# A fifth place for raw weights, paid for with the memory of the first norm's two vectors

## The chip, the cores and the metric

The kernel runs on one core of a Trainium2 chip. The metric is the device time of one execution in microseconds (us), as the median over runs. The engines are named as in the profile: PE is TensorE (PEld its weight loads), DVE VectorE, ACT ScalarE, POOL GpSimd, SP SyncE, which here does little but issue transfers. `L302` is line 302 of the kernel before.

## The reference

One decoder layer on 512 tokens of width 1024 in float32, cut to what matters:

```python
f = swiglu(rms_norm(h, ffn1_norm_pre), gate1, up1, down1)      # 1024 -> 2816 -> 1024
h = h + 0.5 * rms_norm(f, ffn1_norm_post)
u = rms_norm(h, mix_norm_pre)
q, k, v, xr, yr, gl = split(u @ w_in)                          # 12 heads of 128; LRU width 1024
attn = dilated_window_attention(q, k, v)                       # 3 groups of 4 heads, mixed by log-sum-exp
rec = rg_lru(causal_conv4(xr)) * gelu(yr)                      # two gates, 4 blocks of 256x256
merged = sigmoid(gl_0) * (attn @ w_attn_branch) + sigmoid(gl_1) * (rec @ w_rec_branch)
h = h + rms_norm(merged @ w_out, mix_norm_post)
f = swiglu(rms_norm(h, ffn2_norm_pre), gate2, up2, down2)
h = h + 0.5 * rms_norm(f, ffn2_norm_post)
```

## The kernel before

**Products.** A float32 product is made of three matmuls on operands that are split into a high and a low part: high times high, high times low, low times high (`mm3`, L314 to L317). The large products use a seven-product form in the manner of Strassen: sums of weight quarters and of activation quarters are multiplied in products p1 to p7. `seventh` (L709 to L717) issues such products with 128x256 matmuls L715, L716, L717; the feed-forward's down projection issues them with 128x512 matmuls L966, L967, L968 in `down7`, called S matmuls below.

**Weights.** All weights come as raw float32 tiles of 128x1024 from one stream `in_w`. `raw_of` (L234) takes a place with the tag `raw`, of which there are four, and SP issues the transfer (L242). A raw tile is split by `split`: ScalarE copies out the high part (L302), VectorE subtracts it to get the low part (L303). For the seven-product form `w_forms` (L671) and `w_forms_within` (L691) make sums first: L678, L679, L680 and L683 on VectorE, some of them in place in the raw tile; `d_forms` (L893) does the same for the down projection, L909 to L923. A raw place is free again when its last split has been done.

**Feed-forward.** The 22 blocks of the hidden width are computed in order, the first ones (six in the first feed-forward, three in the second) in the standard form (`std_out`, L853, which in the first feed-forward scales by the norm's vector `r1` on the way out), the others in the seven-product form. For the down projection they are cut into five parts of four, four, four, four and six blocks. The first four, a0 to a3, use the seven-product form; the last is multiplied in the ordinary way. The down projection of each of a0 to a3 goes in four steps i0 to i3, interleaved with the gate and up products of the next blocks (`prod`, L866). A step i computes the products `SEVEN_STEPS[i]`: p1 and p7; p4 and p6; p5; p2 and p3. `down7` (L957) collects each in one of three `aux` banks of PSUM, ScalarE first puts the chain sum into the bank (`seed`, L955) where one exists, and evacuates it (L971) into `facc` or into `ea`, a tile `[128, 4, 2, 512]` with the tag `e` of the pool `act1`, which `seed` allocates (L951). `copy` (L729) evacuates the gate and up products.

**Mixer.** Each of four head indices has three heads (one of each dilation). Their scores use an exchange by matmul (L1314), transposes (L1340, L1358, L1363) and softmax operations on VectorE and ScalarE (L1343, L1349, L1352), interleaved with the next products (operands `rb`). In the recurrence the convolution is L1466 and L1469, the gate's two products are L315 and L316 on `rec`, and the gating is L1541 to L1543.

**Order.** A framework schedules the program at build: it fixes one order for each engine from the program's order, priorities and the number of places of each tag. `tc.high_priority(offset=AHEAD)` (100) pulls raw transfers, sums and splits ahead, `EVAC` (200) evacuations. So a place more for a tag changes the built order of engines, not only the waits in it. At run time each engine keeps its order and waits on semaphores.

**First norm.** `acc` (sum of squares) and `r1` (the reciprocal root) are two tiles `[128, 512]` of a pool of their own, `npool`. The first weight block (k = 0) of the start lands in the left part of `first_t`, whose right part `sm` holds small vectors; the blocks k = 1 to 7 land in the halves of four raw places, in which the left half of the first stays empty (`fetch_start`, L277).

Of the kernel before, what the change touches and what calls it, by code (L numbers as in the profile page):

```python
# [10 lines left out]
F32 = mybir.dt.float32  # L11
# [5 lines left out]
P = 128  # L17
T = 512
# [11 lines left out]
EPS = 1e-6  # L30
HB = 256
RAW_W = 1024
NEG = -1.0e30

FIRST_ON = {1: 5, 2: 5}
# [67 lines left out]
def stream_plan():  # L103

    plan = []

    def down(n, a, half):
        for kk in range(part_blocks(a)):
            plan.append((("down", n, a, half, kk), 1024))

    def ffn(n):
        for ev in ffn_order(n):
            if ev[0] == "std":
                plan.append((("gate", n, ev[1]), 1024))
                plan.append((("up", n, ev[1]), 1024))
            elif ev[0] == "prep":
                plan.append((("gu", n, ev[1]), 2048))
            elif ev[0] == "prepd":
                for q in SEVEN_RAW[ev[2]]:
                    plan.append((("dq", n, ev[1], q), 1024))  # L120
        for half in range(2):
            down(n, len(FF_PARTS) - 1, half)

    def qk(h):
        for g in range(NG):
            plan.append((("pair", g * 4 + h, 12 + g * 4 + h), 2048))

    ffn(1)
    del plan[:4]
    for k in range(KC):  # L130
        plan.insert(k, (("start", k), 512))
    for k in range(4):
        plan.append((("v", 0, k), 1024))
    for q in ("g0", "g1", "u0", "u1"):
        plan.append((("vq", q), 2048))
    for h in range(NH):
        qk(h)
    for c in range(0, KC, 2):
        plan.append((("pair", 52 + c, 53 + c), 2048))
    for m in range(0, KC, 2):  # L140
        plan.append((("attn", m), 1024))
    for what, h in LRU_ORDER:
        if what == "gates":
            plan.append((("lru", h), 1024))
        elif (what, h) in PAIRED:
            plan.append((pair_key(what, h), 2048))
        else:
            for c in GATE1[h] if what == "gate1" else (2 * h, 2 * h + 1):
                plan.append((("in", COLUMN[what] + c), 1024))
    for m in range(KC):  # L150
        plan.append((("rec", m), 1024))
    for half in range(2):
        for kk in range(4):
            plan.append((("out", half, kk), 1024))
    ffn(2)

    return [(key + (i,), RAW_W) if width > RAW_W else (key, width)
            for key, width in plan for i in (("lo", "hi") if width > RAW_W else ("",))]


def stream_groups():

    groups, cur, w = [], [], 0
    for key, width in stream_plan():
        if w + width > RAW_W or (cur and cur[0][0][0] == "start"):
            groups.append(cur)
# [12 lines left out]
SMALL_W = _o  # L179
# [4 lines left out]
def hybrid_layer(ctx: ExitStack, tc: tile.TileContext, xT: bass.AP, xN: bass.AP, wst: bass.AP,  # L184
# [4 lines left out]
    cpool = ctx.enter_context(tc.tile_pool(name="cpool", bufs=1))  # L189
    bpool = ctx.enter_context(tc.tile_pool(name="bpool", bufs=6))  # L190
    wpool = ctx.enter_context(tc.tile_pool(name="wpool", bufs=4))
    tpool = ctx.enter_context(tc.tile_pool(name="tpool", bufs=4))
    npool = ctx.enter_context(tc.tile_pool(name="npool", bufs=1))
    psum = ctx.enter_context(tc.tile_pool(name="psum", bufs=1, space=bass.MemoryType.PSUM))
    dpool = ctx.enter_context(tc.tile_pool(name="dpool", bufs=1, space=bass.MemoryType.DRAM))

    first_t = cpool.tile([P, 512 + SMALL_W], F32, name="first")
    sm = first_t[:, 512:]
    cst = cpool.tile([P, CONST_W], F32, name="cst")
    ones = cpool.tile([P, P], F32, name="ones")  # L200
    eps = cpool.tile([P, 1], F32, name="eps")
# [6 lines left out]
    def hm(m, sl=slice(0, T)):  # L208

        return hs["t"][m // 4][:, m % 4, sl]  # L210
# [23 lines left out]
    def raw_of(key, dst=None):  # L234

        g, i = state["g"], state["i"]
        grp = groups[g]
        if i == 0:
            w = grp[-1][1] + grp[-1][2]
            raw = dst if dst is not None else wpool.tile([P, RAW_W], F32, name="raw", tag="raw", bufs=4)  # L240
            src = bass.AP(tensor=wst.tensor, offset=wst.offset + state["off"], ap=[[w, P], [1, w]])
            nc.sync.dma_start(raw[:, :w], src)  # L242
            state["raw"] = raw
            state["off"] += w * P
        k, o, w = grp[i]
        assert k == key, (k, key)
        src = state["raw"][:, o:o + w]
        if i + 1 == len(grp):
            state["g"], state["i"] = g + 1, 0
        else:  # L250
            state["i"] = i + 1
        return src

    def raw_two(key, dst=None):

        return [raw_of(key + (n,), None if dst is None else dst[:, i * RAW_W:(i + 1) * RAW_W])
                for i, n in enumerate(("lo", "hi"))]

    def fetch(key, slot=None, ahead=0):

        with tc.high_priority(offset=ahead if slot else state["ahead"]):
            src = raw_of(key)
            w = src.shape[-1]
            t = slot() if slot else w8() if w > 512 else w4()
            split(t[:, 0, :w], t[:, 1, :w], src)
            return t[:, 0, :w], t[:, 1, :w]

    def w8():
        return wpool.tile([P, 2, 1024], F32R, name="w8", tag="w8", bufs=4)
# [6 lines left out]

    def fetch_start():  # L277

        raws = [wpool.tile([P, RAW_W], F32, name="raw", tag="raw", bufs=4) for _ in range(4)]
        wts = []  # L280
        for k in range(KC):
            raw = raws[k // 2][:, (k % 2) * 512:(k % 2) * 512 + 512]
            if k == 0:
                raw = first_t[:, :512]
                nc.sync.dma_start(hm(k), xT[k])
                nc.sync.dma_start(raw, first[:, :512])
            else:
                nc.sync.dma_start(raw, bass.AP(tensor=wst.tensor, offset=wst.offset + (k - 1) * 512 * P,
                                               ap=[[512, P], [1, 512]]))
                nc.sync.dma_start(hm(k), xT[k])  # L290
            if k % 2 == 0:
                wt = w8()
            o = (k % 2) * 512
            wts.append((wt[:, 0, o:o + 512], wt[:, 1, o:o + 512], raw))
        state["g"], state["off"] = KC, (KC - 1) * 512 * P
        return wts
# [8 lines left out]
    def acc_ps():  # L305
        return psum.tile([P, T], F32, name="acc", tag="acc", bufs=5)
# [138 lines left out]
    def gains(pool, *ids):  # L445

        t = pool.tile([P, 2, D], F32, name="gains", tag="wd", bufs=1)
        for j, i in enumerate(ids):
            nc.gpsimd.dma_start(t[:, j, :], bass.AP(tensor=rows.tensor, offset=rows.offset + i * D,
                                                    ap=[[0, P], [1, D]]))  # L450
        return t[:, 0, :], t[:, 1, :]
# [104 lines left out]
    def act_of(his, los):  # L556
        return Act([his[k // 4][:, k % 4, :] for k in range(8)], [los[k // 4][:, k % 4, :] for k in range(8)])
# [460 lines left out]
    def act_two(pool):  # L1018

        ts = [pool.tile([P, 4, T], F32R, name="xf", tag="xf", bufs=4) for _ in range(4)]  # L1020
        return ts[:2], ts[2:]
# [12 lines left out]
    ap1 = ff1.enter_context(tc.tile_pool(name="act1", bufs=1))  # L1034
    new_h()
    u1 = act_of(*act_two(ap1))
    acc = npool.tile([P, T], F32, name="acc", tag="acc", bufs=1)
    nc.scalar.dma_start(sm, first[:, 512:])
    warm(eps)

# [1 line left out]
    for _ in range(WARM):  # L1042
        PE.matmul(wu[:, :P], ones, ones, start=True, stop=True)
    wts = fetch_start()
    pss = [acc_ps() for _ in range(4)]
    r1 = npool.tile([P, T], F32, name="r", tag="r", bufs=1)
    for k in range(KC):
        wh, wl, raw = wts[k]
        if k == 0:
# [570 lines left out]
    grow5, _ = gains(ap2, 4)  # L1620
# [19 lines left out]
def _bucket(dist):  # L1640
    nf = np.maximum(dist, 1).astype(np.float32)
    large = 16 + (np.log(nf / np.float32(16.0)) / np.float32(math.log(2048 / 16)) * np.float32(16)).astype(np.int32)
    large = np.minimum(large, 31)
    return np.where(dist < 16, dist, large)


def _bias(table):
# [10 lines left out]
    for hd in range(NH):  # L1658
        for g, (sl, s, d, m) in enumerate(((slice(0, 256), s0, 1, m0), (slice(256, 384), s1, 4, m1),
                                           (slice(384, 512), s1, 4, m2))):  # L1660
            vals = table[:, g * 4 + hd][_bucket(np.maximum(s, 0) * d)]
            res[hd, :, sl] = np.where(m, vals, np.float32(NEG))
    return res
# [95 lines left out]
```

## Time and profile before

| what | value |
|---|---|
| median of 3 runs | 1215.21 us (1214.78 to 1215.22) |
| span of the profiled execution | 1213.2 us |
| time outside that span, as median less span | about 2.0 us |
| granted TensorE clock | 0.9 or more of full speed in every slice |
| transfers in all | 149.83 MB, mean 124 GB/s |

The profiled execution is recorded by its span, the time from the first instruction to the last; no other time of that execution is given, so the median stands beside it. Busy time of matmuls is modelled at their ends, so a matmul's duration in the profile is longer than its pitch: what counts is the distance from one start to the next.

### The profile page before, as it was taken

To read this page: it belongs to the slowest core of one execution; us is meant where nothing else is said; L and a number is where in the kernel's file an instruction comes from. 1 tells how busy PE (TensorE), PEld (TensorE's weight loads), DVE (VectorE), ACT (ScalarE), POOL (GpSimd) and SP (SyncE) were. 2 spreads that over 40 slices of the span, in tenths; PEclk is the share of its full clock that TensorE was granted. 3 is DMA by queue.
4 is the path that set the end of the run, shared out by engine and by line. 5 is a ranking of instruction groups with operands and counts; after the bars stand their busy time and mean duration, and the time that the engine had idled before them with its cause. 6 is when DMAs were issued, how large, how long until landed. Compare 5 with 4: busy or idle time off the path is not lost.

```text
span 1213.2 us, 19767 instructions
## 1 busy us (share of the span) xinstructions
PE 1203.3 (99%) x7754; PEld 1099.5 (91%) x7754; DVE 1010.1 (83%) x1536; ACT 815.9 (67%) x1393; POOL 26.1 (2%) x51
## 2 busy tenths in 40 slices
PE   9999999999999999999999999999999999999997
PEld 8899999999888999999989888888899999999996
DVE  7999888989689888888767899875799888889964
ACT  6566787887566565566735898844566677878763
POOL 0000000000011000000000000000100000000000
PEclk9999999999999999999999999999999999999999
DMA  7233333334624232222213342235443333433341
GB/s 266 87 102 125 123 139 111 135 120 155 245 109 143 83 100 96 71 96 87 91 67 123 130 148 88 90 119 179 152 140 110 120 136 107 137 115 129 123 173 70
DMA packets 45822, 149.83 MB, mean 124 GB/s; under 512 B 5152, under 2 KB 8608, under 8 KB 45728
## 3 DMA queue, kind: packets, MB, share of 16 engines
q1 hardware_dynamic: 38160, 131.09, 31.9%
q0 software_dynamic: 7280, 17.30, 4.3%
q8 instruction: 61, 1.00, 0.3%
q14 instruction: 33, 0.27, 0.1%
q10 hardware_dynamic: 288, 0.17, 0.0%
HBM read 138.06 MB, written 6.29 MB: 119 GB/s over the span
## 4 chain that ended last, share of the span: by engine, by line
PE 91%; DVE 5%; DMA 2%; ACT 1%; issue 1%; DVEq 0%
PE acc L715 14%; PE acc L716 14%; PE acc L717 14%; PE acc L315 7%; PE acc L317 7%; PE acc L316 7%; PE aux L966 4%; PE aux L967 3%; PE aux L968 3%; DVE w L303 2%; PE acc L433 2%; PE acc L431 2%; PE acc L432 2%; DMA raw<-in_w 2%; PE aux L433 1%; PE aux L431 1%
## 5 line engine op out<-in xcount | busy, mean ns | idle before, releaser
L717 PE MATMUL acc<-big,w 128*128 128x256 f32 x1240 | 351.8, 284 | 0.0
L715 PE MATMUL acc<-big,w 128*128 128x256 f32 x1240 | 351.6, 284 | 0.0
L716 PE MATMUL acc<-big,w 128*128 128x256 f32 x1240 | 351.3, 283 | 0.0
L303 DVE TENSOR_TENSOR w<-raw,w 128x1024 fp32r<-128x1024 f32 (+1 forms) x272 | 298.2, 1100 | 48.1 <-ACT w L302 41.3
L302 ACT ACTIVATE w<-raw 128x1024 fp32r<-128x1024 f32 (+1 forms) x272 | 259.7, 958 | 100.1 <-PE acc L317 44.9
L715 PEld LDWEIGHTS acc<-big,w 128*128 128x128 f32 x1240 | 237.6, 192 | 2.0
L716 PEld LDWEIGHTS acc<-big,w 128*128 128x128 f32 x1240 | 237.6, 192 | 1.7
L717 PEld LDWEIGHTS acc<-big,w 128*128 128x128 f32 x1240 | 237.7, 192 | 0.0
L966 PE MATMUL aux<-w,xf 128*128 128x512 f32 x224 | 87.5, 393 | 0.8 <-ACT w L302 0.7
L967 PE MATMUL aux<-w,xf 128*128 128x512 f32 x224 | 87.5, 391 | 0.0
L968 PE MATMUL aux<-w,xf 128*128 128x512 f32 x224 | 87.2, 389 | 0.0
L303 DVE TENSOR_TENSOR w<-s,w 128x1024 fp32r<-128x1024 f32 x51 | 62.4, 1223 | 3.7 <-ACT w L302 3.5
L302 ACT ACTIVATE w<-s 128x1024 fp32r<-128x1024 f32 x51 | 54.0, 1058 | 12.6 <-PE acc L717 9.2
L315 PE MATMUL acc<-xf,w 128*128 128x512 f32 (+1 forms) x168 | 59.1, 354 | 0.0
L316 PE MATMUL acc<-xf,w 128*128 128x512 f32 (+1 forms) x168 | 58.6, 350 | 0.0
L317 PE MATMUL acc<-xf,w 128*128 128x512 f32 (+1 forms) x168 | 58.5, 349 | 0.0
L729 ACT ACTIVATE c<-acc 128x256 f32<-128x256 f32 x74 | 28.2, 383 | 41.8 <-PE acc L717 41.8
L966 PEld LDWEIGHTS aux<-w,xf 128*128 128x128 f32 x224 | 41.9, 188 | 9.6 <-ACT w L302 1.3
L968 PEld LDWEIGHTS aux<-w,xf 128*128 128x128 f32 x224 | 42.1, 188 | 8.8
L315 PE MATMUL acc<-big,w 128*128 128x512 f32 x128 | 49.8, 389 | 0.0
L316 PE MATMUL acc<-big,w 128*128 128x512 f32 x128 | 49.8, 389 | 0.0
L317 PE MATMUL acc<-big,w 128*128 128x512 f32 x128 | 49.8, 389 | 0.0
(436 smaller groups left out, 2745.7 us busy)
## 6 DMA issues: line engine op xcount, KB each, us to landing
raw<-in_w SPq DMA_DIRECT2D x232, 512.0 KB, 3.5
big<-xf POOLq DMA_DIRECT2D x6, 512.0 KB, 3.9
gains<-in_rows POOLq DMA_DIRECT2D x5, 512.0 KB, 5.8
h<-in_x SPq DMA_DIRECT2D x8, 256.0 KB, 5.1
h<-in_xn POOLq DMA_DIRECT2D x4, 512.0 KB, 6.2
kept_m<-h POOLq DMA_DIRECT2D x4, 512.0 KB, 2.9
vals<-in_w SPq DMA_DIRECT2D x4, 512.0 KB, 5.9
h<-kept_m POOLq DMA_DIRECT2D x4, 512.0 KB, 5.4
```

What stands on the lines that cost most here:

```text
L302: state["split"] = ACT.activation(dh, src, AF.Copy).ins
L303: DVE.tensor_sub(dl, src, dh.bitcast(F32))
L315: PE.matmul(ps, wh, xh, start=first, stop=False)
L316: PE.matmul(ps, wh, xl, start=False, stop=False)
L317: PE.matmul(ps, wl, xh, start=False, stop=last)
L431: PE.matmul(ps, x.hi[k][:, bl], wh, start=k == 0 and not seeded, stop=False, skip_group_check=True)
L715: PE.matmul(ps, wh, xh, start=start and k == 0, stop=False, skip_group_check=True)
L716: PE.matmul(ps, wh, xl, start=False, stop=False, skip_group_check=True)
L717: PE.matmul(ps, wl, xh, start=False, stop=k == 3, skip_group_check=True)
L966: PE.matmul(ps, xh, wh, start=first and j == 0, stop=False, skip_group_check=True)
L967: PE.matmul(ps, xh, wl, start=False, stop=False, skip_group_check=True)
L968: PE.matmul(ps, xl, wh, start=False, stop=j == 1, skip_group_check=True)
```

## The change

There are five raw places instead of four (4 KiB more on each partition). To pay for it, `npool` is gone: `acc` and `r1` become the halves of one tile `[128, 2, 512]` that takes the tag `e` of `act1`, the slot in which the chain sums `ea` are put later. `first_t` loses its left part, and the weight block k = 0 lands in the empty left half of the first raw place.

```diff
+RAW_N = 5
...
-    npool = ctx.enter_context(tc.tile_pool(name="npool", bufs=1))
...
-    first_t = cpool.tile([P, 512 + SMALL_W], F32, name="first")
-    sm = first_t[:, 512:]
+    sm = cpool.tile([P, SMALL_W], F32, name="first")
...
-            raw = dst if dst is not None else wpool.tile([P, RAW_W], F32, name="raw", tag="raw", bufs=4)
+            raw = dst if dst is not None else wpool.tile([P, RAW_W], F32, name="raw", tag="raw", bufs=RAW_N)
...
-        raws = [wpool.tile([P, RAW_W], F32, name="raw", tag="raw", bufs=4) for _ in range(4)]
+        raws = [wpool.tile([P, RAW_W], F32, name="raw", tag="raw", bufs=RAW_N) for _ in range(4)]
...
             if k == 0:
-                raw = first_t[:, :512]
                 nc.sync.dma_start(hm(k), xT[k])
                 nc.sync.dma_start(raw, first[:, :512])
...
-    acc = npool.tile([P, T], F32, name="acc", tag="acc", bufs=1)
+    norm = ap1.tile([P, 2, T], F32, name="acc", tag="e", bufs=1)
+    acc, r1 = norm[:, 0], norm[:, 1]
...
-    r1 = npool.tile([P, T], F32, name="r", tag="r", bufs=1)
```

## The prediction

> **What bounds the kernel now.** I read the page first: the engine shares, the chain that ended last, and the groups.
>
> ```profile
> span 1213.2 us, 19767 instructions
> PE 1203.3 (99%) x7754; PEld 1099.5 (91%) x7754; DVE 1010.1 (83%) x1536; ACT 815.9 (67%) x1393; POOL 26.1 (2%) x51
> PE 91%; DVE 5%; DMA 2%; ACT 1%; issue 1%; DVEq 0%
> L966 PE MATMUL aux<-w,xf 128*128 128x512 f32 x224 | 87.5, 393 | 0.8 <-ACT w L302 0.7
> ```
>
> TensorE is busy for 1203.3 of 1213.2 us and carries 91% of the chain. The change takes no matmul away, so the time can fall only by what is left of waiting in TensorE's stream. The group of L966 shows the size of such waits: 0.8 us of idle before 224 matmuls. Small as they are, they are the whole of what can move. The median of the runs is 1215.21 us, the profiled span 1213.2, so about 2.0 us lies outside the span; I work on the span and add those 2.0.
>
> The second view is that of the waits, first of all engines, then of SP's queue, because the change concerns the places that weights land in.
>
> ```profile
> DVE s L679 <- DMA raw<-in_w: 15.7, 16, 1.7
> DVE s L678 <- DMA raw<-in_w: 8.9, 9, 1.8
> SPq L242 <- DVE w L303: 655.9, 154, 19.4
> ```
>
> SP stands for 655.9 us (154 times) with a transfer that could start but for a place, which VectorE's split (L303) has not yet freed: places are short. VectorE in turn waits 15.7 + 8.9 = 24.6 us in 25 waits for raw weights that have not landed. That is what a fifth place can take away. But VectorE is at 83%, and TensorE at 99% beside it, so hardly any of the 24.6 us reaches TensorE. The question is which of them do. I looked at that in the chain of waits, stretch by stretch, and went through TensorE's timeline for starts that come later than the pitch (0.12 us for 256 columns, 0.23 for 512, rows below).
>
> One place where a raw transfer does end up in TensorE's stream is in the first feed-forward:
>
> ```profile
> 91.19 5.75 DMA raw<-in_w
> 97.03 0.69 DVE s L679
> 97.72 0.47 DVE raw L680
> 98.66 1.13 DVE w L303
> ...
> 100.48 1.05 ACT w L302
> 101.53 0.49 ACT facc L971
> 102.06 0.50 PE aux L966
> ```
>
> The raw pair lands at 96.94; VectorE's sums and split, ScalarE's split and its evacuation (L971) follow one another without a gap, and L966 starts last.
>
> **What the change does, in order of program.** The instructions are the same in number on TensorE, VectorE, ScalarE and GpSimd. The memory: the first norm's `acc` and `r1` go into the slot of `ea`. Their last readers are the standard outputs of the first feed-forward, which precede the first write of `ea` in the order of both kernels, so I cost this at nothing; the start chunk k=0 only goes to another address. What matters is the built order, which differs: with one place more the scheduler puts the raw transfers and VectorE's sums L678, L679 and L680 some 2 to 20 places earlier, and as a result moves 139 matmuls.
>
> *Hoisted pairs.* In the first feed-forward's down projection, the first two L966 of the last step (i3) of parts a0, a1 and a2 now stand 72 to 74 places earlier, in the middle of the next product, right behind the last S matmuls of step i2 and twelve 256-wide ones. The kernel before has that same shape in its second feed-forward, and there it waits:
>
> ```profile
> 1018.20 0.60 ACT ea L971
> 1018.80 0.96 ACT w L302
> ```
> ```profile
> 1019.32 0.28 PE L717 MATMUL acc<-big,w 128*128 128x256 f32 x1
> 1019.80 0.73 PE L966 MATMUL aux<-w,xf 128*128 128x512 f32 x2 [0.20 <-ACT w L302]
> 1020.37 0.28 PE L715 MATMUL acc<-big,w 128*128 128x256 f32 x1
> ```
>
> ScalarE needs 0.60 for the evacuation and 0.96 for the split, 1.56 us, where twelve matmuls give 12 x 0.12 = 1.44 of cover; the wait is 1019.80 - 1019.32 - 0.12 = 0.36 us. The pair then takes 0.57 instead of 2 x 0.23 = 0.46: 0.11 more. One hoisted pair costs 0.47 us. In the first feed-forward, second part, today:
>
> ```profile
> 165.94 0.62 ACT L302 ACTIVATE xf<-tt 128x512 fp32r<-128x512 f32 x1
> 166.46 0.58 ACT L971 ACTIVATE ea<-aux 128x512 f32<-128x512 f32 x1
> 166.93 1.05 ACT L302 ACTIVATE w<-raw 128x1024 fp32r<-128x1024 f32 x1
> ```
> ```profile
> 165.93 0.28 PE L715 MATMUL acc<-big,w 128*128 128x256 f32 x1
> 167.36 0.28 PE L715 MATMUL acc<-big,w 128*128 128x256 f32 x1
> ```
>
> In the new order the weight split follows L971 directly. The last S matmul starts a pitch before 165.93 and ends near 166.1, so `w` is there at 166.1 + 0.58 + 1.05 = 167.7, while the twelve matmuls end at 167.36: again some 0.35 of wait and 0.11 behind it. I take 0.47 for each of the three pairs: +1.41 (from 0, if ScalarE is ahead there, to 1.2 for the first pair, which could wait for the whole of L971 and L302 with little cover).
>
> *What they leave.* In the first part the late L966 of 102.06 is gone from that place, and with it the transfer's wait:
>
> ```profile
> 101.57 0.39 PE L968 MATMUL aux<-w,xf 128*128 128x512 f32 x1
> 102.06 0.50 PE L966 MATMUL aux<-w,xf 128*128 128x512 f32 x1
> 102.40 0.39 PE L967 MATMUL aux<-w,xf 128*128 128x512 f32 x1
> ```
>
> 102.06 comes 0.49 behind, 102.40 another 0.34: 0.26 + 0.11 = 0.37 over the pitch of 0.23. The transfer of 91.19 now gets its place some 3 us earlier, more than VectorE's wait of 1.7. A matmul behind it (109.19) is late by a small amount as well, which I put at 0.10 as a guess: -0.47. In the second feed-forward one pair (first part, i2) goes back from the middle of a product to its end:
>
> ```profile
> 946.91 0.73 PE aux L966 x2
> ```
>
> The chain has it behind ScalarE's evacuation and split just as at 1019.80, so at the same price: -0.47. The two other pairs of that kind in the second feed-forward stay.
>
> *Recurrence gates.* The largest single wait on TensorE is here:
>
> ```profile
> 685.19 0.60 DVE gt L1541
> ...
> 686.49 0.02 ACT rec L302
> ...
> 687.02 1.05 ACT w L302
> ```
> ```profile
> 688.12 0.73 PE L315 MATMUL aux<-rec,w 128*128 128x512 f32 x2 [1.50 <-ACT w L302]
> ```
>
> VectorE's chain of L1469, L1541 and L1543 ends at 686.47 and ScalarE follows. In the new order one L1541 leaves that chain, 0.60 with its pause 0.64: -0.64. In the first gate it is the other way round:
>
> ```profile
> 658.61 0.69 DVE L303 TENSOR_TENSOR rec<-sig,rec 128x512 fp32r<-128x512 f32 x1 [0.57 <-ACT rec L302]
> 660.03 0.40 PE L315 MATMUL aux<-rec,w 128*128 128x512 f32 x1
> ```
>
> The lower half of `rec` is ready at 659.30 and TensorE comes at 660.03. Two more 512-wide operations (a split and L700) now stand ahead of it on VectorE; at 0.69 each it is ready at 660.68, with the restart +0.75 (0 if VectorE has caught up thanks to earlier weights, 1.4 if neither is hidden).
>
> *Attention.* In each of four heads the block of exchange, transposes and L1358/L1363 is placed 16 to 25 matmuls earlier, with five breaks into the product instead of six.
>
> ```profile
> 497.30 0.21 PE acc L717
> ```
> ```profile
> 461.22 0.28 PE L715 MATMUL acc<-big,w 128*128 128x256 f32 x1
> 461.58 0.30 PE L1340 MATMUL aux<-cst,facc 128*128 128x128 f32 x1
> 500.52 0.28 PE L716 MATMUL acc<-rb,w 128*128 128x256 f32 x1
> 500.81 0.63 PE L1340 MATMUL aux<-cst,facc 128*128 128x128 f32 x4
> ```
>
> A break costs 0.21 - 0.12 = 0.09. The last transposes come 0.36 behind (0.24 over the pitch) in the first head and 0.29 behind (0.17) in the second. With these gone, and a break, a head gains 0.17 to 0.26; I take 0.21 for three heads and 0.29 for the first: -0.92. That holds if VectorE is earlier by as much as TensorE's block, 16 x 0.12 = 1.9 us and more: out of its way go one L679, one L680 and one L303, 0.69 + 0.47 + 1.13 = 2.29 us by the rows from 97.03 on. That is enough with 0.1 to 0.4 to spare, which is little.
>
> **Sum.** +1.41 - 0.47 - 0.47 + 0.75 - 0.64 - 0.92 = -0.34 us: a span of 1212.9 and a time of 1214.9. A difference of 0.2%, 2.43 us, is about what a measurement of this kernel can tell from no change; below 1212.8 I call it faster, above 1217.6 slower.
>
> [...]
>
> **The rivals.**
> [...] If earlier raw weights let ScalarE make every `w` in time, the three new pairs cost nothing, nor does the first gate: -0.34 - 1.41 - 0.75 = -2.5 us, and with the two pairs that stay in the second feed-forward (2 x 0.47) -3.4: 1211.8 to 1212.7. For it: 24.6 us of VectorE's waits for transfers. Against it: 166.46, where ScalarE's evacuation depends on TensorE's own last matmul and no earlier transfer helps. 0.18.
> *VectorE comes late for attention.* If it frees less than the 2 us by which TensorE's block has been moved, because L678 and L679 of the pair after, now earlier, stand in front of the softmax's operations, every head waits. The price is up to 2 us a head; with 1 us each, +4.0, and the gain of 0.92 is lost: +4.6, 1219.8. It decides from a shortage of 0.8 us a head on, which carries the sum past 2.43. For it: the spare of 0.1 to 0.4. Against it: both estimates are of order and rows that hardly vary. 0.14.
> *Hoisted sums wait for their transfer.* L679 placed up to 20 operations earlier stands in VectorE's queue until its raw tile lands (5.75 us at 91.19), and all behind it stand too, evacuations of the products among them. Two such waits of 1.7 us that reach TensorE give +3.4 - 0.3 = +3.1: 1218.3. 0.09.
> *Nothing.* Transfers are hidden and the moved matmuls cancel to the last tenth: 1215.2. 0.09.
>
> **How the numbers follow.** The forecast as summed has 0.50, with its own range from 1212.8 (no pair costs more than 0.1, the gate half) to 1217.2 (first pair 1.2 instead of 0.47, no gain in attention nor in the second gate: -0.34 + 0.73 + 0.92 + 0.64 = +1.95). The range of 8 in 10 reaches into the rivals on both sides: 1212.2 to 1217.8. Same is 0.50 + 0.09 and a little of the faster rival, 0.60; faster 0.17; slower 0.14 + 0.09 = 0.23.
>
> **What would show it.** In the profile after: L966 some 0.2 idle behind ACT w L302 three times in the first feed-forward; no wait of the chain on raw<-in_w near 91 to 97; the idle time before L315 of the second gate about 0.9 where its row has 1.50, that of the first gate about 0.7; the waits of DVE s L678 and L679 for transfers well under 24.6 us with TensorE's busy time unchanged. Wrong would be: waits of L1314, L1340 or L1358 for VectorE (then attention decides), or L966 without waits (then ScalarE was ahead), or VectorE's waits for transfers as long as before.

## The result, and the profile after

The changed kernel takes 1220.60 us (median of 5 runs, 1219.95 to 1221.76) against 1215.21 (1214.44 to 1215.81): a ratio of 1.0046, 95% interval 1.0033 to 1.0058. It is slower by 5.4 us, outside the forecast range. The profiled execution is the longest of the five: it took 1221.76, of which 1220.0 is the span; the others had spans from 1218.2 to 1219.1.

The page of the kernel after, with the lines that answer to those of before (line numbers are lower by one or two: L964 to L966 were L966 to L968, L300 and L301 were L302 and L303, L676 to L678 were L678 to L680):

```profile
span 1220.0 us, 19771 instructions
...
PE 1206.2 (99%) x7754; PEld 1101.2 (90%) x7754; DVE 1010.6 (83%) x1536; ACT 816.8 (67%) x1393; POOL 26.2 (2%) x51
...
PE 87%; DVE 6%; ACT 3%; DMA 2%; issue 1%; DVEq 0%; ACTq 0%
...
L964 PE MATMUL aux<-w,xf 128*128 128x512 f32 x224 | 87.4, 394 | 2.5 <-ACT w L300 2.3
```

The busy shares hardly move, and TensorE still stands at 99%. What moves is the chain, from 91% to 87% TensorE, and the idle time before L964, from 0.8 to 2.5 us behind ScalarE's split. The waits for transfers show where the fifth place helped and where it did not:

```profile
DVE s L676 <- DMA raw<-in_w: 8.8, 4, 4.1
...
DVE raw L916 <- DMA raw<-in_w: 8.2, 5, 3.1
DVE s L677 <- DMA raw<-in_w: 8.0, 9, 1.7
ACT w L300 <- DMA raw<-in_w: 7.6, 2, 3.9
```

Before, VectorE's sums had waited 25 times for raw weights, at most 1.8 us each. Now these sums wait 13 times, but up to 4.1 us, and a sum that had hardly waited before is among them (L916: 8.2 us, 0.7 then). All in all VectorE waits 25.0 us for raw weights, against 25.7 before (24.6 in the sums, 1.1 elsewhere): in the new order the fifth place takes next to nothing off its waits.

To see where the time went I took, in both traces, every start of a matmul on TensorE less the start ahead of it and less the pitch (0.120 us for 256 columns, 0.227 for 512 and 0.11 for 128, the medians of these distances in both traces; for the sixteen matmuls of 16 or 32 columns a value of 0.06 that I set, the same for all kernels), and summed this excess by stretch of the program. The stretches are bounded by the same numbers of matmuls in all kernels; the times are those of before. The last column is experiment e5, below.

| stretch, us of before | before | after | e5 |
|---|---|---|---|
| start to 95 | 2.97 | 3.22 | 2.71 |
| 95 to 116, first part, steps i0 to i3 | 0.62 | 0.48 | 0.01 |
| 157 to 175 and 217 to 235, parts a1 and a2 | 0.04 | 0.98 | 0.04 |
| 433 to 447, first scores | 0.74 | 1.47 | 0.73 |
| 447 to 583, four heads | 4.66 | 4.34 | 4.61 |
| 632 to 646, ahead of the gates | 0.13 | 0.65 | 0.13 |
| 646 to 667, first gate | 0.01 | 0.56 | 0.01 |
| 667 to 697, second gate | 1.79 | 3.91 | 1.80 |
| 909 to 957, second feed-forward, a0 | 0.51 | 0.05 | 0.51 |
| 1051 to 1121, second feed-forward, from a2 on | 0.74 | 3.37 | 0.71 |
| whole span | 14.44 | 21.27 | 13.59 |

21.27 - 14.44 = 6.83 us is the whole difference of the two spans (1220.0 - 1213.2). Of it, 1.5 us are a lower clock behind the second gate (0.50 from 692.82 to 696.23), which not every execution has (last section); the 5.3 that are left are close to the 5.4 between the medians. The first row is not a loss of its own: between before and e5, whose orders are the same, the start differs by as much (2.97 and 2.71). The waits themselves, in the timeline of TensorE of the kernel after:

```profile
107.92 0.50 PE L964 MATMUL aux<-w,xf 128*128 128x512 f32 x1 [0.21 <-ACT w L300]
167.83 0.50 PE L964 MATMUL aux<-w,xf 128*128 128x512 f32 x1 [0.20 <-ACT w L300]
227.74 0.50 PE L964 MATMUL aux<-w,xf 128*128 128x512 f32 x1 [0.20 <-ACT w L300]
442.06 0.38 PE L1292 MATMUL aux<-qk 128*128 128x128 f32 x1 [0.51 <-DVE facc L1273]
642.42 0.39 PE L713 MATMUL acc<-rb,w 128*128 128x256 f32 x1 [0.39 <-ACT acc L727]
662.50 0.50 PE L313 MATMUL aux<-rec,w 128*128 128x512 f32 x1 [0.28 <-ACT w L300]
689.96 0.73 PE L313 MATMUL aux<-rec,w 128*128 128x512 f32 x2 [0.77 <-ACT w L300]
691.82 0.50 PE L314 MATMUL aux<-rec,w 128*128 128x512 f32 x1 [1.13 <-DVE rec L301]
1086.26 0.73 PE L964 MATMUL aux<-w,xf 128*128 128x512 f32 x2 [1.49 <-ACT w L300]
1106.79 0.39 PE L713 MATMUL acc<-big,w 128*128 128x256 f32 x1 [0.37 <-ACT c L727]
```

The first three are the hoisted pairs, with the wait that was forecast. Those at 442, 642, 691 and 1106 weren't in the forecast, and that at 1086 was there before with a sixth of the idle time it has now (0.24 us).

### The profile page after: what moved, and what is told of

Read it like the earlier page. It is cut to its first block, busy times and chain, and to the rows that moved or that the text cites. A ratio compares the mean times of both kernels' runs of the same rounds, so it can differ in the third digit from the quotient of the medians.

```text
span 1220.0 us, 19771 instructions
## 1 busy us (share of the span) xinstructions
PE 1206.2 (99%) x7754; PEld 1101.2 (90%) x7754; DVE 1010.6 (83%) x1536; ACT 816.8 (67%) x1393; POOL 26.2 (2%) x51
## 4 chain that ended last, share of the span: by engine, by line
PE 87%; DVE 6%; ACT 3%; DMA 2%; issue 1%; DVEq 0%; ACTq 0%
PE acc L713 13%; PE acc L714 13%; PE acc L715 13%; PE acc L313 7%; PE acc L314 7%; PE acc L315 7%; PE aux L964 4%; PE aux L965 4%; PE aux L966 4%; DVE w L301 3%; DMA raw<-in_w 2%; PE acc L429 2%; PE acc L431 2%; PE acc L430 2%; ACT w L300 1%
## 5 line engine op out<-in xcount | busy, mean ns | idle before, releaser
L301 DVE TENSOR_TENSOR w<-raw,w 128x1024 fp32r<-128x1024 f32 (+1 forms) x272 | 297.3, 1098 | 69.1 <-ACT w L300 68.2
L300 ACT ACTIVATE w<-raw 128x1024 fp32r<-128x1024 f32 (+1 forms) x272 | 259.8, 958 | 107.6 <-PE acc L315 43.4
L964 PE MATMUL aux<-w,xf 128*128 128x512 f32 x224 | 87.4, 394 | 2.5 <-ACT w L300 2.3
L966 PE MATMUL aux<-w,xf 128*128 128x512 f32 x224 | 87.2, 389 | 0.0
L301 DVE TENSOR_TENSOR w<-s,w 128x1024 fp32r<-128x1024 f32 x51 | 62.1, 1219 | 2.4 <-ACT w L300 2.4
L300 ACT ACTIVATE w<-s 128x1024 fp32r<-128x1024 f32 x51 | 53.8, 1055 | 9.7 <-PE acc L715 6.5
L313 PE MATMUL acc<-xf,w 128*128 128x512 f32 (+1 forms) x168 | 59.3, 355 | 0.0
L314 PE MATMUL acc<-xf,w 128*128 128x512 f32 (+1 forms) x168 | 58.7, 350 | 0.0
L964 PEld LDWEIGHTS aux<-w,xf 128*128 128x128 f32 x224 | 41.8, 188 | 11.5 <-ACT w L300 3.3
L966 PEld LDWEIGHTS aux<-w,xf 128*128 128x128 f32 x224 | 42.1, 188 | 8.8
L313 PE MATMUL acc<-big,w 128*128 128x512 f32 x128 | 49.8, 389 | 0.0
L314 PE MATMUL acc<-big,w 128*128 128x512 f32 x128 | 49.8, 389 | 0.0
```

The costliest lines, as they stand in the source:

```text
L300: state["split"] = ACT.activation(dh, src, AF.Copy).ins
L301: DVE.tensor_sub(dl, src, dh.bitcast(F32))
L313: PE.matmul(ps, wh, xh, start=first, stop=False)
L314: PE.matmul(ps, wh, xl, start=False, stop=False)
L964: PE.matmul(ps, xh, wh, start=first and j == 0, stop=False, skip_group_check=True)
L966: PE.matmul(ps, xl, wh, start=False, stop=j == 1, skip_group_check=True)
```

## The experiments

Theory A: the fifth place and the moved memory cost nothing; the loss comes from the order that the scheduler builds when it has five places. Rival B: the moved memory costs. Rival C: a fifth place in use costs by itself. Others are named where they arise. All ratios are to the kernel before, run beside each experiment.

**e1: the moved memory alone.** With four places the built order is that of before on every engine.

```diff
-RAW_N = 5
+RAW_N = 4
```

> The changed kernel with four raw places again; the norm's vectors stay in the slot of the chain sums and the first weight block stays in the first raw place. The built order of every engine is that of the kernel before. Theory A (the loss comes from the order that five places give): 1215.2 us, within 0.1% of before, with the same waits on TensorE (1.66 us over the pitch at the second gate, none of 1.3). Rival B (the moved memory costs): 1218 or more, most of the 5.4 us.

Measured: 1215.47 us, ratio 1.000 (0.9992 to 1.0009). The memory of the two vectors and of the first weight block costs nothing; B falls. The trace has the waits of before at the gates (1.81 of excess at the second), but not the one at 102 us: L964 to L966 follow one another at the pitch there, with four places and the order of before.

```profile
101.86 0.39 PE L966 MATMUL aux<-w,xf 128*128 128x512 f32 x1
102.09 0.39 PE L964 MATMUL aux<-w,xf 128*128 128x512 f32 x1
102.32 0.39 PE L965 MATMUL aux<-w,xf 128*128 128x512 f32 x1
```

The transfer ahead of it took 4.44 us here and 5.75 in the profile before, and VectorE waited 0.42 us for it instead of 1.73. So four places alone don't make the wait at 102 us; in the profile before it stands behind a transfer that took 1.3 us longer.

**e2, e3 and e4: one of the five places held, stage by stage.** A dummy takes a raw place and keeps it until a late operand is read.

```diff
+    def hold(ap):
+        t = wpool.tile([P, RAW_W], F32, name="held", tag="raw", bufs=RAW_N)
+        DVE.tensor_copy(t[:, :1], ap)
+        return t
...
+    held2 = hold(u2.hi[0][:, 384:385].bitcast(F32))
     end2 = ffn(2, u2, None, forms_of(u2, his, los, ap2, True), ap2, pss)
+    end_hold(held2, end2[2].hi[-1][:, :1].bitcast(F32))
```

> The changed kernel, but one of the five raw places is held by a dummy from the start of the second feed-forward to the end of its products; the order there is that of before, elsewhere that of the changed kernel. Theory A, by the sums of TensorE's waits in the two traces: the second feed-forward gives back 2.63 us of new waits (1068 to 1107) and loses the 0.46 gained at 947: 1220.6 - 2.2 = 1218.4 us. Rival C (a fifth place costs by itself wherever it is used, by transfers in each other's way): a share by time, 280 of 1213 us, so 1.2 us: 1219.4, and waits left in the second feed-forward.

Measured: 1219.07 us, ratio 1.0031 (1.0019 to 1.0043). That is 1.5 us less than the changed kernel and lies between the two numbers, nearer to C's, so the time alone does not tell them apart. The trace speaks for A: the excess from 1051 on falls from 3.37 to 0.94, and that at 909 to 957 goes back to 0.50.

> The changed kernel, but one of the five raw places is held by a dummy from the first value products to the end of the merged gates; the order of attention and gates is that of before. Theory A: waits of 0.73 (442), 0.52 (642), 0.55 (662) and 2.12 (690 to 692) go, the 0.32 gained in attention too: 1220.6 - 3.6 = 1217.0 us. Rival C: a share by time, 500 of 1213 us, 2.2 us: 1218.4.

> Both holds: five places are in use in the first feed-forward alone. Theory A: only the start (+0.25) and the three hoisted pairs (+0.94, less 0.14) are left of the change: 1216.3 us, 1.1 above before. Rival C: 1217 or more. Rival D (the first feed-forward is where the loss starts and everything behind it only shifts): 1219 or more.

Measured: 1225.48 (ratio 1.0083) and 1225.79 (1.0086), both slower than the changed kernel, where all theories had said faster. In e3's trace the gates and the heads have the waits of before again, as A says (1.81 at the second gate), but the stretch of the value products ahead of them has 7.00 of excess instead of 0.80 (the kernel's lines stand nine higher in this run):

```profile
348.38 0.50 PE L1132 MATMUL acc<-w,big 128*128 128x512 f32 x1 [1.63 <-ACT w L309]
393.33 0.50 PE L1176 MATMUL aux<-w,rb 128*128 128x512 f32 x1 [2.86 <-DVE rb L310]
```

The dummy, taken at that very place, moved four splits of the value weights about 50 places back in VectorE's order. So the experiment brought a disorder of its own and says nothing on the time of the rest. The runs below prescribe the order instead.

**e5: five places with the order of before.** The edit prescribes the issue order of each engine by dependencies of the class `NoSync`. No added wait shows on TensorE: its excess in e5 is 13.59 us, against 14.44 before. A table gives the order of before for the 7626, 1536 and 1273 instructions of TensorE, VectorE and ScalarE.

```diff
         hybrid_layer(tc, *args)
+        in_order(tc, nc)
...
+def in_order(tc, nc):
+    traced = list(nc.cur_bb.bb.instructions)
+    for engine, text in ORDER.items():
+        own = [i for i in traced if str(i.engine) == "EngineType." + engine]
...
+                tc.add_manual_dep(own[n], last.name, mybir.DependencyInfo(
+                    mybir.DependencyClass.NoSync, mybir.DependencyReason.DATA), reason="order")
```

> Five raw places as in the changed kernel, but the orders of TensorE, VectorE and ScalarE are prescribed, instruction by instruction, to be those of the kernel before; nothing else differs from the changed kernel. Theory A (the order costs): 1215.2 us or up to 0.6 less, since the wait at 102 us, ended by a transfer that can now start earlier, may go (0.37). The new waits at 442, 642, 662, 691 and 1068 to 1107 are gone. Rival C (a fifth place in use costs by itself): 1218 to 1220.

Measured: 1214.24 us, ratio 0.9990 (0.9981 to 0.9999). C falls, and A holds. The wait at 102 us is gone here too, but e1 and e10 lack it with four places, so its going isn't shown to be the fifth place's doing.

```profile
102.00 0.39 PE L966 MATMUL aux<-w,xf 128*128 128x512 f32 x1
102.22 0.39 PE L964 MATMUL aux<-w,xf 128*128 128x512 f32 x1
102.45 0.39 PE L965 MATMUL aux<-w,xf 128*128 128x512 f32 x1
```

In its list of waits no row is left of an engine waiting for `raw<-in_w`. So with the order of before the fifth place does take away all of VectorE's 24.6 us, and the kernel gains at most about 1 us by it. The 6.4 us between e5 and the changed kernel come from the order and what it brings.

**e6, e7, e11 and e12: the new order in one stage alone.** The table takes one stretch from the built order of the changed kernel, on all three engines, and all else from that of before.

```diff
-ORDER = order of before
+ORDER = order of before, with the stretch of one stage from the order of the changed kernel
```

> As e5_five_old_order, with the changed kernel's order on the three engines in the first feed-forward alone. By the traces the three hoisted pairs cost 0.47 each there (107.9, 167.8, 227.7): +1.4 us over e5 (1214.24), 1215.7. If hoisted pairs cost nothing once the fifth place is in use: as e5.

Measured: 1215.93 us, ratio 1.0005 (0.9996 to 1.0014), 1.7 us over e5. The pairs wait as in the changed kernel:

```profile
167.10 0.72 PE L964 MATMUL aux<-w,xf 128*128 128x512 f32 x2 [0.21 <-ACT w L300]
227.00 0.72 PE L964 MATMUL aux<-w,xf 128*128 128x512 f32 x2 [0.21 <-ACT w L300]
```

> As e5_five_old_order, with the changed kernel's order on the three engines in the attention stage alone (about 425 to 585 us). By the traces: +0.73 for the wait of L1292 at 442, -0.32 for the earlier exchange and transposes: +0.4 us over e5, 1214.6. By the prediction's own term: -0.92, 1213.3. If VectorE comes late in every head: 1217 or more.

Measured: 1214.59 us, ratio 0.9992 (0.9983 to 1.0001), 0.35 over e5. The trace has the wait of L1292 at the start of the stage, and little gained in the heads (4.24 of excess against 4.61):

```profile
440.00 1.16 PE L1292 MATMUL aux<-qk 128*128 128x128 f32 x8 [0.57 <-DVE facc L1273]
```

> As e5_five_old_order, but with the changed kernel's order on the three engines in one stretch alone, the recurrence gates (about 630 to 710 us). Theory A, from the two traces: waits of 0.52 at 642, 0.55 at 662, and 0.92 + 1.30 instead of 1.66 at 690: +1.6 us over e5, 1216.8, and now and then up to 1.5 more, if the clock of TensorE is lowered behind the two waits as it was in the profile of the changed kernel. Rival E (an early shift of everything behind makes the waits, not the order at the place): as e5.

Measured: 1215.79 us, ratio 1.0006 (0.9997 to 1.0015), 1.55 over e5, as expected (the expectations of e6 and e7 counted e5 as 1215.2); rival E falls. Both waits of the second gate come with the order:

```profile
687.48 0.73 PE L313 MATMUL aux<-rec,w 128*128 128x512 f32 x2 [0.77 <-ACT w L300]
689.34 0.50 PE L314 MATMUL aux<-rec,w 128*128 128x512 f32 x1 [1.13 <-DVE rec L301]
```

> As e5_five_old_order, but with the changed kernel's order in the second feed-forward alone. Theory A: +0.89 + 1.24 + 0.50 (waits of 1068 to 1107) - 0.46 (the pair at 947): +2.2 us over e5, 1217.4. Rival E: as e5.

Measured: 1215.00 us, ratio 0.9996 (0.9988 to 1.0005), 0.8 over e5: the right sign and a third of the size. VectorE's waits for transfers are back, from none in e5,

```profile
DVE s L676 <- DMA raw<-in_w: 9.6, 3, 4.4
DVE raw L916 <- DMA raw<-in_w: 5.2, 4, 1.4
```

and TensorE waits behind them: 0.36 us at 1039.20, 0.51 at 1079.55 where the changed kernel had 1.49, and 0.37 at 1100.11 as there. So the same order of instructions in this stage cost 1.6 us of excess here and 2.6 there. One difference is on record: the transfer ahead of L916 at 1060.30 took 5.82 us in the changed kernel, and VectorE waited 3.06 for it; no wait of L916 in e7 is over 1.4. Whether that is the reason isn't shown.

Every run of e6, and of e11 (on another chip), is longer than every run of e5, so these two stages cost something; the runs of e7 and e12 overlap with those of e5, and for them the traces count more than the time. The four stages together, 1.7 + 0.35 + 1.55 + 0.8 us, are 4.4 of the 6.4 us, though they hold nearly all that differs in the orders. The other 2.0 show only with the whole order. The difference in the second feed-forward is a part of them; the clock behind the second gate (last section) may be another; the rest is open.

**e9: which engine's order.** VectorE and ScalarE have the order of the changed kernel, TensorE that of before. (The reverse, TensorE's new order with the old one of the others, wasn't tried.)

> Five raw places; VectorE's and ScalarE's orders are those of the changed kernel, TensorE's is prescribed to be that of the kernel before. If VectorE's order is what costs at the gates and in the second feed-forward: those waits stay, the three hoisted pairs of the first feed-forward go (-0.94), the pair at 947 comes back (+0.46): 1220.1 us by that count, and between 1218.5 and 1220.5, since attention's exchange stands 2 us later again. If TensorE's own order is what costs (matmuls moved ahead of their operands): near e5_five_old_order, 1214 to 1216.

Measured: 1219.54 us, ratio 1.0031 (1.0019 to 1.0043). About two thirds of the loss (0.31% of 0.46%) stay without one matmul of TensorE having been moved. e9 prescribes its orders by the same means as e5, so these means are not what makes e5 faster. At the gates and in the second feed-forward the waits are those of the changed kernel:

```profile
691.42 0.50 PE L314 MATMUL aux<-rec,w 128*128 128x512 f32 x1 [1.10 <-DVE rec L301]
1085.93 0.50 PE L964 MATMUL aux<-w,xf 128*128 128x512 f32 x1 [1.16 <-ACT w L300]
```

In the first feed-forward the three pairs wait no more, but TensorE's excess there is as large as in the changed kernel (1.5 us from 95 to 235): other matmuls wait in their place, the longest for ScalarE at 112.18. With the new order of VectorE and ScalarE, putting the pairs back gains nothing.

**e8 and e10: a better order, with five places and with four.** In the table of e5, the matmuls that stand early in the middle of another product and wait there go back behind it; the change of the table, in words:

```diff
-  p5 of one step in the second feed-forward (three times): L966, L966 ... 72 matmuls ... L967, L968, L967
+  72 matmuls, L966, L967, L968, L966, L967, L968 (the same for L315 and L316 of two gates)
```

> As e5_five_old_order, with those matmuls put back into the places of the program that stand early in the middle of another product and wait there: three pairs of L966 in the second feed-forward (947, 1019, 1079: 0.47 each) and the first L315 and L316 of the first two gates (688: 1.77). Theory A, extended (TensorE's order against what its operands' makers can do is all that is left to gain): 1215.2 - 1.4 - 1.8 = 1212.0 us. Rival F (a wait that is taken away comes back at the next matmul that needs the same operands): within 0.5 of e5.

> As e8_five_unhoisted (prescribed order of before, early matmuls put back), with four raw places instead of five. What the fifth place is worth when the order does not change with it: theory A says 0.6 us, the wait at 102 us: 1213.7. If the fifth place brings nothing, 1213.1; if VectorE's waits for transfers (24.6 us with four places) matter once TensorE waits less elsewhere, 1214.5 or more.

Measured: 1213.11 us, ratio 0.9982 (0.9973 to 0.9991), and 1213.36, ratio 0.9986 (0.9977 to 0.9995). Both are faster than either kernel of this study. The three pairs of the feed-forward gave back what was expected (the excess of 909 to 957 falls from 0.51 to 0.05, that of 999 to 1029 from 0.50 to 0.03), so rival F falls there. At the second gate it holds: the wait moved on to the next product that needs ScalarE.

```profile
689.54 0.39 PE L713 MATMUL acc<-rb,w 128*128 128x256 f32 x1 [1.04 <-ACT acc L727]
692.93 0.38 PE L713 MATMUL acc<-big,w 128*128 128x256 f32 x1 [0.27 <-ACT c L727]
```

In e10 VectorE waits 15.0 + 10.8 us for raw weights in L677 and L676, in e8 not at all, and the two times differ by 0.25 us. That is the fifth place's worth in this order, too little to tell from nothing.

## Why the prediction was wrong

Term by term, the forecast against the excess of the profiles (kernel after less kernel before):

| term | forecast | measured, us |
|---|---|---|
| three hoisted pairs | +1.41 | +1.41 |
| wait at 102, first feed-forward | -0.47 | -0.61 |
| pair at 947, second feed-forward | -0.47 | -0.46 |
| first gate | +0.75 | +0.55 |
| second gate | -0.64 | +0.6, and 1.5 of clock |
| attention, four heads | -0.92 | -0.32 |
| first scores, at 442 | none | +0.73 |
| ahead of the gates, at 642 | none | +0.52 |
| second feed-forward from a2 on | none | +2.63 |
| start | none | +0.25 |
| sum | -0.34 | +6.8 |

**What held.** The change acts through the built order, as the text argued; the moved memory, put at nothing, costs nothing (e1). *Hoisted pairs*: the wait of 0.36 and the 0.11 behind it were met three times, and e11 shows +1.7 us for that stage. (The working, 1.56 less 1.44 of cover, gives only 0.12 of wait; the price came from the timeline, and that reading held.) The pair at 946.91: 0.51 became 0.05. The row of the second gate, "about 0.9": 0.77 idle.

**What came out by luck.** *The wait at 102 us*: it went, but e1 and e10 are without it too, with four places; the price rested on one transfer of 5.75 us in one execution. *First gate*: the size is near, but the operand is another. The text had the lower half of `rec` come last, from VectorE. It is ready at 662.51, in time for L314 at 662.84; L313 at 662.50 waits for ScalarE's split of the weights, which stands behind the high half of `rec`. The two operations that the text named do stand ahead on VectorE and stand in front of both halves.

**Where it failed.** Three steps, and two terms left out. The text also took the 0.8 us of idle before L966 for the size of TensorE's waits; over the pitch, its starts add up to 14.4 us before.

*Recurrence gates, second.* The term was -0.64: one L1541 leaves the chain that ends in ScalarE's split. It did leave it, with an L1540 in its place, and the first wait fell from 1.66 to 0.92 us; but I followed the high half of `rec` alone. The low half, VectorE's own split, went two places back in the same order, behind L1539 and L1549:

```profile
687.63 0.66 DVE sig L1467
688.29 1.02 DVE xr L1464
689.31 0.52 DVE gt L1539
...
690.48 0.68 DVE th L1549
691.16 0.61 DVE rec L301
```

L314, the second matmul of that product, waits for it until 691.82, 1.30 us over the pitch. So the term is 0.92 + 1.30 + 0.11 instead of 1.66 + 0.11: +0.6, and e6 shows it. The other 1.5 us in that stretch are the clock (below).

*"The two other pairs of that kind in the second feed-forward stay."* TensorE's places stay, and I priced them as unchanged. What feeds them didn't stay. Most of the sums L676 and L677 stand earlier in VectorE's order, by up to 14 places, and VectorE stands still ahead of them until the raw weights are there (1.67 us at 1079.13). The chain of the kernel after:

```profile
1074.62 4.42 DMA raw<-in_w
...
1079.13 0.69 DVE s L677
...
1080.76 1.13 DVE w L301
...
1082.59 1.05 ACT w L300
1083.63 0.49 ACT ea L969
...
1084.75 0.52 ACT ea L969
1085.26 0.95 ACT w L300
```
```profile
1079.13 0.69 DVE L677 TENSOR_TENSOR s<-s,raw 128x512 f32<-128x512 f32 x1 [1.67 <-DMA raw<-in_w]
```

The transfer starts when a place is freed at 1074.60 and takes 4.42 us; VectorE has other work for a part of it and then stands idle for 1.67. Before, the same sum waited 1.37 us for its transfer too, but after L683, L878, L873 and two splits. Now it stands ahead of them, and all of them come late (L681, L876, L871 here), then ScalarE, then TensorE at 1086.26. This is the rival "hoisted sums wait for their transfer", priced at +3.4 us of waits with a chance of 0.09; here the stage is worth 2.63, of which the order alone, in e7, brought 1.6. It should have had the larger chance, since the order of VectorE with these sums pulled ahead was known, and so was the landing time of 5.75 us. That the scheduler, with more places, takes the sums' operands to be there earlier than they are is a guess at its reasons; what is shown is the order and its price.

*Attention*, -0.92: measured -0.32 in the heads. Where L1340's last wait of 0.17 went, L1312 (L1314 before), now earlier, comes 0.24 over the pitch, at 496.71; VectorE writes its operand at 496.40 to 496.56. The block was moved ahead of what VectorE could deliver, though by far less than the rival feared.

*Left out.* The +0.73 of L1292 at 442 is the same mechanism as in the second feed-forward: VectorE's sums L677 and L678 now stand ahead of the first scores, and L677 waits 1.37 us for its transfer.

```profile
432.75 3.46 DMA raw<-in_w
...
436.31 0.06 DVE s L677
...
436.92 1.22 DVE w L301
...
442.06 1.05 PE aux L1292 x7
```

The +0.52 at 642 was left out too: ScalarE takes a split (0.62 us from 639.53) ahead of the first half of a Gelu (0.63 from 641.47), and the evacuation that TensorE needs (642.00) comes behind both.

**The rivals.** That TensorE would stop waiting fell with the three pairs. That VectorE would be late in every head fell with e12. "Nothing" fell with the result. The slower side came out by one of the two smallest of the four chances, together with terms that weren't in the sum. The forecast's own range ended at 1217.2, because its upper end added up the worst of the terms that I had and no term for a place that I had not looked at; the stated 1217.8 leaned on the rivals. One limit of theirs doesn't follow from the sum: with attention's gain of 0.92 lost, a shortage of 0.46 us in each of four heads would have carried it past 2.43, not 0.8.

## What to carry to other kernels

One more buffer can make a kernel slower where the program's order is made by a scheduler that knows of the buffer (here 1215.21 us became 1220.60, and 1214.24 with the order of before): compare the orders, and for each operation that moves ahead ask whether its operand has landed, and what stands behind it on its engine (the sum at 1079.13 waited 1.67 us). Follow both halves of a split, and every operand of a matmul, not only the one that was last before (at the second gate the half that I left out cost 1.30 us). To find out whether a resource or the order it induces is at fault, run the new resource with the old order prescribed.

## What the runs showed of the hardware

The profile of the kernel after lost 1.5 us to TensorE's clock. The windows view has for each engine its busy time and the number of instructions that reach into the stretch, then the granted clock (the third value from the end of a row) and the DMA share; here the stretch behind the two waits of the second gate in the kernel after, and the same stretch in e2, whose waits there are as long (0.92 and 1.30 over the pitch in both):

```profile
690.00:692.70 2.70, 1.57 (x8) 1.10 (x9) 2.70 (x4) 1.43 (x3) 0.00 (x0) 1.00 0.00 0
692.80:696.20 3.40, 3.40 (x18) 3.40 (x18) 3.40 (x7) 1.42 (x3) 1.12 (x2) 0.50 0.54 161
```
```profile
692.80:696.20 3.40, 3.40 (x30) 3.40 (x30) 3.40 (x7) 1.81 (x4) 1.12 (x2) 1.00 0.51 161
```

At a granted clock of 0.50 the kernel after has 18 matmuls in the 3.40 us, e2 30 in the same time. The low clock lasts from 692.82 to 696.23, 3.41 us, and its matmuls of 256 columns start 0.213 us apart, where the pitch is 0.120; over the sixteen of them that makes the 1.5 us. e9 has the fall too: its windows view gives 0.50 from 692.0 to 695.2, with 17 matmuls in the 3.20 us. e2 and e6 have the pair of waits without the fall: 1.00 in the row of e2 above, and a mean clock of 1.000 over the whole profiled execution of e6 (0.998 in the kernel after and in e9).

So in two of the four profiled executions with this pair of waits, the place cost twice: the waits themselves and, in the kernel after, 1.5 of the 3.41 us behind them. That the waits bring the fall about is my inference from where it stands, 1.00 us after the start of L314 at 691.82. Why two of the executions kept their clock over waits as long isn't shown.
